# Storing GDN's Sm matrices as two transfers of 64 rows, with four Sm tiles

## The chip, the cores and the metric

The kernel runs on one core of one Trainium2 chip. The metric is device time in microseconds (us) for one execution. The kernel before has a median of 1775.48 us over three runs (1773.43 to 1786.22).

## The reference, cut to what matters

The reference is a two-layer trunk for a flow-matching generator: 256 latent tokens and 256 context tokens, model width 1024. Each layer runs four token mixers side by side (RWKV-7, gated DeltaNet or GDN, GLA and windowed attention), merges them by sigmoid gates, and ends with a SwiGLU. All of it is float32. The change touches GDN alone. For every chunk of 64 tokens, every head (four) and both directions GDN builds a strictly triangular matrix and solves with it:

```python
decay = jnp.exp(jnp.where(causal, gc[..., :, None] - gc[..., None, :], -jnp.inf))
lmat = jnp.where(strict, beta[..., :, None] * jnp.einsum('bnhid,bnhjd->bnhij', k, k) * decay, 0.0)
m = lmat + jnp.eye(c, dtype=F32)
u = lax.linalg.triangular_solve(m, v * beta[..., None], left_side=True, lower=True, unit_diagonal=True)
```

There are 512 tokens, so 8 chunks, 4 heads and 2 directions: 64 matrices of 64 x 64 in each layer. RWKV-7 is computed in the same chunked way and has matrices of the same size to invert.

## The kernel before, in words

Everything is issued by hand-written Python in program order, and a planner (the Tile layer) decides at build time in which order each engine runs its instructions. It goes by priorities: parts inside `high_priority(offset=20000)` come first, the gate projections (`w_gate`) are put late, to fill TensorE where other work waits. It also places tiles in memory pools. A tile with a tag has `bufs` slots; a new tile of that tag can only be written once the users of the slot's earlier tile are done, a DMA that reads it among them. At run time each engine works through its own list strictly in order, and so does SP, whose queue issues every DMA of this kernel. A wait at the head of a list holds all that stands behind it.

A layer runs RWKV (lines 372 to 600), then GDN (from line 625), with attention and GLA in the gaps. Beside them the dense projections run: each loads a 512 KB weight block `raw` (line 1111), ACT makes its rounded high part `whi`, DVE the rest `wlo`, and TensorE does 24 or so matmuls `pd` from both.

GDN's preparation makes the matrices in lines 740 to 764. Its outer loop runs over b, the pairs of heads. TensorE makes the Gram matrices of all eight chunks in one PSUM tile `pr` (traced as `m`), head p = 0 of the pair on partitions 0 to 63 and head p = 1 on 64 to 127. The inner loop runs over the direction d: DVE multiplies `pr` with minus beta into the tile `Sm` [128, 8, 64], then with the decays `At`. `Sm` has the tag "Sm" in the pool `gdt`, which has two slots for each tag. Four `Sm` tiles are made in each layer, in the order (b, d) = (0,0), (0,1), (1,0), (1,1). Line 764 then stores one tile to the DRAM scratch `dl`, whose dimensions are [j 64, d 2, p 2, b 2, n 8, i 64]. The stored access is `j p n i -> p j (n i)`: its first dimension is p with 2 steps, then j with 64, then 2 KB in a row. It is one transfer of 256 KB.

`tri_inverse` (lines 295 to 365) reads `dl` back in another order: two loads into `lx` (d = 0), two into `lt` (d = 1, line 314) and four into `bt` (line 318), in 32 x 32 blocks, one matrix to a lane. DVE then copies and runs 30 elimination steps on `lt` and `lx`, the result goes to DRAM and back as `TT`, and GDN's chain over the chunks (`gchain`, matmuls `psc`) uses it.

RWKV stores its matrices with the helper `tri_put` (line 291): `self.nc.sync.dma_start(out=st[0][:, d, p, b], in_=s)`. There s has the 64 partitions of one head, so the first dimension on both sides is j with 64 steps, again with 2 KB in a row: 128 KB for one transfer, 16 of them in the two layers.

Of the kernel before, what the change touches and what calls it, by code (L numbers as in the profile page):

```python
# [7 lines left out]
F32 = mybir.dt.float32  # L8
# [110 lines left out]
def bc(ap, shape, axis):  # L119
    return ap.unsqueeze(axis).to_broadcast(shape)  # L120


class Kern:
# [508 lines left out]
    def gdn(self, l, getp, misc, sg, y, full, other=lambda: None, fill=lambda: None, pre=None):  # L632
        nc, P, Q = self.nc, self.P, self.Q
        q0 = 0 if full else 256
        qs = 0 if full else 4
        with ExitStack() as es:
# [4 lines left out]
            tmp = self.pool("gdt", 2, es=e1, side="right")  # L641
# [15 lines left out]
            st = self.tri_begin()  # L657
# [41 lines left out]
            for p in range(2):  # L699
                for d in range(2):  # L700
                    nc.sync.dma_start(out=qi[64 * p:64 * p + 64, d].rearrange("p b t -> p (b t)"),
                                      in_=grd[p, d, 2 * d:2 * d + 2].rearrange("b n i -> (b n i)").partition_broadcast(64))
# [3 lines left out]
            for m in range(4):  # L706
                d = m % 2
# [37 lines left out]
            for b in range(2):  # L745
                for d in range(2):
                    EG = c3(qi[:, d, b])
                    Dd = At[:, d, b]
                    self.tt(Dd, EG, bc(GC[:, d, :, b], [128, 8, 64], 2), ALU.subtract)
                    self.act(EG, EG, ACTF.Exp)  # L750
                    nc.gpsimd.tensor_copy(el[:, d, b], EG[:, :, 63 if d == 0 else 0])
                    self.tt(c3(ke[:, d, b]), c3(QK[:, b, 0]), EG)
                    self.tt(Dd, Dd, bc(gmask[:, d], [128, 8, 64], 1), ALU.min)
                    self.act(Dd, Dd, ACTF.Exp)
                pr = self.ps().rearrange("p (n i) -> p n i", i=64)
                for n in range(8):
                    tk = slice(64 * n, 64 * n + 64)
                    for rw in rws:
                        self.mm(pr[rw, n], QK[rw, b, 0, tk], QK[rw, b, 0, tk])
                for d in range(2):  # L760
                    Sm = tmp.tile([128, 8, 64], F32, tag="Sm", name=self.nm("Sm"))
                    self.tt(Sm, pr, bc(nB[:, :, 2 * d + b], [128, 8, 64], 2))
                    self.tt(Sm, Sm, At[:, d, b])
                    nc.sync.dma_start(out=st[0][:, d, :, b].rearrange("j p n i -> p j (n i)"), in_=Sm.rearrange("p n i -> p (n i)"))
            next(inv)
            for b in range(2):
                conv(f"gq{b}", b, QK[:, b, 1, q0:T], q0)
# [78 lines left out]
            for s in range(8):  # L846
                with HP():
                    got = lockstep([link(s, d) for d in range(2)])
                for d in range(2):
                    n, U, So = got[d]  # L850
# [964 lines left out]
```

## Time and profile before

| | |
|---|---|
| median of three runs | 1775.48 us |
| the profiled execution | 1780.3 us, span 1778.5 us |
| TensorE (PE) busy | 1653.0 us, 93% of the span |
| VectorE (DVE) busy | 1097.3 us, 62% |
| ScalarE (ACT) busy | 831.2 us, 47% |
| mean granted TensorE clock | 0.961 of full speed |
| DMA queue 1 | 261.69 MB, 46.8% of 16 engines' span |

The span is cut into instructions per engine; PEld is the weight load of TensorE, which overlaps its matmuls. An idle stretch of an engine is put down to what ended it (the releaser). The chain of waits follows the end of the program back from each instruction to what released it. A DMA share is the mean busy share of the 16 DMA engines, so 0.06 is one engine and 1.00 all of them.

### The profile page before, as it was taken

To read this page: it belongs to the slowest core of one execution; us is meant where nothing else is said; L and a number is where in the kernel's file an instruction comes from. 1 tells how busy PE (TensorE), PEld (TensorE's weight loads), DVE (VectorE), ACT (ScalarE), POOL (GpSimd) and SP (SyncE) were. 2 spreads that over 40 slices of the span, in tenths; PEclk is the share of its full clock that TensorE was granted. 3 is DMA by queue.
4 is the path that set the end of the run, shared out by engine and by line. 5 is a ranking of instruction groups with operands and counts; after the bars stand their busy time and mean duration, and the time that the engine had idled before them with its cause. 6 is when DMAs were issued, how large, how long until landed. Compare 5 with 4: busy or idle time off the path is not lost. (4 is left out here: it accounts for less than half of the span.)

```text
span 1778.5 us, 31562 instructions
## 1 busy us (share of the span) xinstructions
PE 1653.0 (93%) x12480; PEld 1321.6 (74%) x12480; DVE 1097.3 (62%) x2243; ACT 831.2 (47%) x1440; POOL 144.1 (8%) x255
## 2 busy tenths in 40 slices
PE   6999999998998989999999999898999868889998
PEld 3776775666786667888878888777777766779986
DVE  3466643447935775899774226666577666766654
ACT  3665442355534235544433217763556432366653
POOL 0000111001001350000000000001021002400000
PEclk8999999998999999999999999998889877989999
DMA  9322554442452372566774223344532463445553
GB/s 338 119 96 90 157 151 164 150 146 78 140 146 90 94 239 90 186 222 216 242 236 153 95 95 107 102 127 136 162 98 97 127 167 103 142 143 187 183 201 118
DMA packets 149684, 263.71 MB, mean 148 GB/s; under 512 B 62224, under 2 KB 77088, under 8 KB 149408
## 3 DMA queue, kind: packets, MB, share of 16 engines
q1 hardware_dynamic: 149536, 261.69, 46.8%
q8 instruction: 98, 1.61, 0.4%
q14 instruction: 50, 0.41, 0.1%
HBM read 236.12 MB, written 25.53 MB: 147 GB/s over the span
## 5 line engine op out<-in xcount | busy, mean ns | idle before, releaser
L193 PE MATMUL pd<-hh,whi 128*128 128x512 f32 (+1 forms) x1648 | 550.8, 353 | 17.3 <-ACT g L171 5.2
L193 PE MATMUL pd<-hl,whi 128*128 128x512 f32 (+1 forms) x1648 | 545.5, 349 | 0.5 <-DVE hl L183 0.5
L183 DVE TENSOR_TENSOR wlo<-raw,whi 128x1024 fp32r<-128x1024 f32 x280 | 342.6, 1225 | 260.7 <-ACT whi L180 105.3
L180 ACT ACTIVATE whi<-raw 128x1024 fp32r<-128x1024 f32 x280 | 296.1, 1058 | 434.1 <-PE pd L193 251.9
L193 PEld LDWEIGHTS pd<-hh,whi 128*128 128x128 f32 x1648 | 317.1, 193 | 72.8 <-issue 9.2
L193 PEld LDWEIGHTS pd<-hl,whi 128*128 128x128 f32 x1648 | 317.2, 193 | 43.6 <-issue 6.1
L193 PE MATMUL pd<-hh,wlo 128*128 128x512 f32 (+1 forms) x1648 | 339.2, 345 | 4.9 <-DVE wlo L183 4.9
L193 PEld LDWEIGHTS pd<-hh,wlo 128*128 128x128 f32 x1648 | 263.5, 190 | 47.2 <-DVE wlo L183 5.3
L193 PE MATMUL t<-whi,ul 128*128 128x512 f32 x264 | 104.6, 396 | 0.0
L193 PE MATMUL t<-whi,uh 128*128 128x512 f32 x264 | 104.2, 395 | 0.0
L1258 DVE SCALAR_TENSOR_TENSOR gr<-gr,crow 128x512 f32<-128x512 f32 x112 | 75.5, 688 | 27.1 <-DMA gr<-in_ada_t_dram 26.1
L193 PE MATMUL t<-wlo,uh 128*128 128x512 f32 x264 | 75.3, 395 | 0.0
L171 ACT ACTIVATE g<-g 128x512 f32<-128x512 f32 (+1 forms) x128 | 66.6, 522 | 2.9
L183 DVE TENSOR_TENSOR th<-th,pd 128x512 f32<-128x512 f32 (+1 forms) x88 | 48.6, 552 | 29.2 <-PE pd L193 27.3
L183 POOL TENSOR_TENSOR acc<-acc,g 128x512 f32<-128x512 f32 (+1 forms) x48 | 57.5, 1215 | 60.7 <-DVE g L183 60.6
L193 PE MATMUL pd<-yp,whi 128*128 128x512 f32 (+1 forms) x192 | 54.0, 388 | 7.1 <-DVE g L183 3.5
L193 PEld LDWEIGHTS t<-whi,ul 128*128 128x128 f32 x264 | 49.7, 188 | 11.7
L193 PEld LDWEIGHTS t<-wlo,uh 128*128 128x128 f32 x264 | 49.7, 188 | 11.7
L193 PEld LDWEIGHTS t<-whi,uh 128*128 128x128 f32 x264 | 49.7, 188 | 11.4 <-DVE yr L183 0.2
L171 ACT ACTIVATE g<-pd,P 128x512 f32<-128x512 f32 (+1 forms) x64 | 36.9, 576 | 44.0 <-PE pd L193 33.1
L180 ACT ACTIVATE uh<-th 128x512 fp32r<-128x512 f32 (+1 forms) x44 | 23.1, 526 | 72.8 <-DVE th L183 72.7
L190 DVE SCALAR_TENSOR_TENSOR ac<-pp,P,ac 128x512 f32<-128x512 f32 (+1 forms) x72 | 52.2, 726 | 1.4 <-POOL UV L505 0.3
(366 smaller groups left out, 2241.1 us busy)
## 6 DMA issues: line engine op xcount, KB each, us to landing
raw<-in_ffn_w_dram SPq DMA_DIRECT2D x132, 512.0 KB, 3.3
raw<-in_w_gate_dram SPq DMA_DIRECT2D x64, 512.0 KB, 3.5
gr<-in_ada_t_dram SPq DMA_DIRECT2D x112, 256.0 KB, 3.4
raw<-in_w_in_dram SPq DMA_DIRECT2D x52, 512.0 KB, 3.3
raw<-in_ada_w_dram SPq DMA_DIRECT2D x40, 512.0 KB, 4.7
gd<-g SPq DMA_DIRECT2D x32, 256.0 KB, 3.2
raw<-in_w_branch_dram SPq DMA_DIRECT2D x16, 512.0 KB, 4.6
g<-gd SPq DMA_DIRECT2D x32, 256.0 KB, 4.2
```

The source lines that it names most:

```text
L171: return self.nc.scalar.activation(out=out, in_=in_, func=func, bias=bias, scale=scale, **kw)
L180: return self.nc.scalar.activation(out=out, in_=in_, func=ACTF.Copy, scale=scale)
L183: return (eng or self.nc.vector).tensor_tensor(out=out, in0=a, in1=b, op=op)
L190: return self.nc.vector.scalar_tensor_tensor(out=out, in0=a, scalar=s, in1=b, op0=op0, op1=op1)
L193: self.last = self.nc.tensor.matmul(out, lhsT=lhsT, rhs=rhs, start=start, stop=stop, skip_group_check=skip)
L1258: nc.vector.scalar_tensor_tensor(out=raw if v == nv - 1 else junk, in0=raw, scalar=1.0, in1=self.cr[:, v, 512 * h:512 * h + 512], op0=ALU. ...
```

## The change

Line 764 is replaced by two calls of RWKV's helper `tri_put`, one for each half of the partitions, so that a tile is stored by two transfers of 128 KB whose first dimension is j with 64 steps. The tag "Sm" gets four slots in place of two, so that all four tiles of a layer have memory of their own; a slot is 2 KB of each partition, and the pool `gdt` grows by 4 KB of each partition. The bytes stored, their places in DRAM and all arithmetic stay as they were. In the two layers 8 transfers become 16.

```diff
-                    Sm = tmp.tile([128, 8, 64], F32, tag="Sm", name=self.nm("Sm"))
+                    Sm = tmp.tile([128, 8, 64], F32, tag="Sm", name=self.nm("Sm"), bufs=4)
                     self.tt(Sm, pr, bc(nB[:, :, 2 * d + b], [128, 8, 64], 2))
                     self.tt(Sm, Sm, At[:, d, b])
-                    nc.sync.dma_start(out=st[0][:, d, :, b].rearrange("j p n i -> p j (n i)"), in_=Sm.rearrange("p n i -> p (n i)"))
+                    for p in range(2):
+                        self.tri_put(st, d, b, p, Sm[64 * p:64 * p + 64])
```

## Rows read from the trace of the kernel before

**Rows 1.** The page: busy time of the engines, and the whole chain by line.
```profile
PE 1653.0 (93%) x12480; PEld 1321.6 (74%) x12480; DVE 1097.3 (62%) x2243; ACT 831.2 (47%) x1440; POOL 144.1 (8%) x255
PE pd L193 12%; PE t L193 5%; PE m L193 2%; PE psc L193 2%; DMA dl<-Sm 1%; DVE wlo L183 1%; DVE lx L183 1%; DMA TT<-dx 1%; DVE lt L183 1%; PE S L193 1%; PE Y L193 0%; DMA dx<-lt 0%; PE O L193 0%; ACT whi L180 0%; SPq L336 0%
```

**Rows 2.** Chain of waits in layer 1: start us, length us, what held the end.
```profile
1391.72 10.57 DMA dl<-Sm
1402.32 0.69 DVE Sm L183
1403.97 9.29 DMA dl<-Sm
1413.68 2.74 DMA lt<-dl
```

**Rows 3.** By stretch: engines' busy us (x), granted PE clock, DMA share, GB/s.
```profile
428.00:430.00 2.00, 2.00 (x9) 1.56 (x10) 0.00 (x0) 0.15 (x1) 0.00 (x0) 1.00 0.13 51
438.00:440.00 2.00, 0.42 (x1) 0.43 (x2) 2.00 (x4) 0.63 (x1) 0.00 (x0) 0.50 0.13 51
1405.00:1407.00 2.00, 2.00 (x31) 1.78 (x32) 1.43 (x6) 0.00 (x0) 0.00 (x0) 0.50 0.13 51
1203.00:1205.00 2.00, 1.94 (x45) 1.63 (x40) 0.88 (x3) 1.76 (x4) 0.62 (x3) 1.00 0.92 304
```

**Rows 4.** The page's DMA issues: count, KB of one, us from issue to landing.
```profile
dl<-XL SPq DMA_DIRECT2D x16, 128.0 KB, 4.5
lx<-dl SPq DMA_DIRECT2D x8, 128.0 KB, 5.9
```

**Rows 5.** VectorE and SP in layer 0: start, us, operation [idle before <-releaser].
```profile
431.25 0.69 DVE L183 TENSOR_TENSOR Sm<-m,nB 128x512 f32<-128x512 f32 x1 [5.01 <-DMA dl<-Sm]
436.31 0.69 DVE L183 TENSOR_TENSOR Sm<-m,nB 128x512 f32<-128x512 f32 x1 [3.11 <-DMA dl<-Sm]
438.17 0.68 DVE L183 TENSOR_TENSOR QK<-tc,ac 128x512 f32<-128x512 f32 x1
423.20 15.57 SPq L764 DMA_DIRECT2D dl<-Sm  x4
446.54 0.91 SPq L314 DMA_DIRECT2D lt<-dl  x2
...
457.05 0.19 DVE L183 TENSOR_TENSOR lx<-lt 128x30 f32<-128x30 f32 x1
```

**Rows 6.** TensorE in layer 0, at full and at half clock.
```profile
419.13 1.02 PE L193 MATMUL m<-sq,c_ones 128*128 128x512 f32 x2
424.99 1.89 PE L193 MATMUL pd<-hh,wlo 128*128 128x512 f32 x7
439.57 2.08 PE L193 MATMUL m<-sq,c_ones 128*128 128x512 f32 x2 [7.38 <-ACT sq L171]
440.66 5.26 PE L193 MATMUL pd<-hh,wlo 128*128 128x512 f32 x12
```

**Rows 7.** VectorE and TensorE in layer 1.
```profile
1397.30 0.69 DVE L183 TENSOR_TENSOR Sm<-m,nB 128x512 f32<-128x512 f32 x1 [4.40 <-DMA dl<-Sm]
1402.32 0.69 DVE L183 TENSOR_TENSOR Sm<-m,nB 128x512 f32<-128x512 f32 x1 [2.53 <-DMA dl<-Sm]
1416.55 0.21 DVE L183 TENSOR_TENSOR lx<-lt 128x30 f32<-128x30 f32 x1 [0.92 <-DMA lt<-dl]
1399.66 0.58 PE L193 MATMUL pd<-hh,whi 128*128 128x256 f32 x1 [4.65 <-ACT g L171]
1401.75 0.41 PE L193 MATMUL pd<-hl,whi 128*128 128x256 f32 x1
1403.49 1.12 PE L193 MATMUL m<-QK 64*64 64x64 f32 x16 [1.32 <-DVE QK L190]
1406.38 2.47 PE L193 MATMUL m<-c_idn,v 64*64 64x64 f32 x64
1411.11 1.35 PE L193 MATMUL pd<-hh,wlo 128*128 128x256 f32 x10
...
1382.25 2.03 PE L193 MATMUL m<-c_idn,QK 64*64 64x64 f32 x64
1380.33 2.08 PE L193 MATMUL m<-QK 64*64 64x64 f32 x64
```

**Rows 8.** SP's queue in layer 1.
```profile
1389.21 3.03 SPq L764 DMA_DIRECT2D dl<-Sm  x2
...
1399.21 0.49 SPq L764 DMA_DIRECT2D dl<-Sm  x1
1407.81 2.29 SPq L314 DMA_DIRECT2D lx<-dl  x2
1433.28 15.08 SPq L1111 DMA_DIRECT2D raw<-in_w_branch_dram  x5
```

## The prediction

> **What bounds the kernel now.** I read the page first. TensorE is busy for 93% of the span and leads the chain of waits, and the store `dl<-Sm` has 1% of that chain, far more than eight transfers of 256 KB should need [rows 1]. So for most of the run the sum of the matmuls decides, and the change can only pay where TensorE stands still, or runs at a lower clock, because of this store. Second, the chain in order of time: in layer 1 it lies on the store for 10.57 us, then 9.29 us [rows 2]. Third, the table by stretches, to see why. In layer 0 and in layer 1 alike the DMA share stands at 0.13 while the four stores run, and 51 GB/s move [rows 3]. 0.13 of 16 engines is two engines. A tile of 262 KB at 51 GB/s takes 5.1 us, four of them 20.6 us, which fits the 20 us from the first issue at 423.2 us to the time at which layer 0's reads of `dl` can go on [rows 5]. The store's first dimension has two steps. RWKV's stores of the same kind of data, with 64 steps first, are landed 4.5 us after issue [rows 4], and the stretch with the last two of them moves 304 GB/s at a share of 0.92 (a weight block is among that traffic) [rows 3]. I conclude that the order of dimensions puts the store on two engines. Fourth, the instructions beside it: VectorE waits for a free Sm tile 5.01 and 3.11 us in layer 0 [rows 5], 4.40 and 2.53 us in layer 1 [rows 7]. What follows it on its list waits too, and so TensorE stands for 7.38 us in layer 0 [rows 6], 4.65 and 1.32 us in layer 1 [rows 7], and restarts at half clock (granted 0.50, the 1.2 GHz level, after it stood) [rows 3].
>
> **The change part by part.**
>
> *Four Sm tiles.* The third and fourth tile no longer wait for the stores of the first and second. VectorE's list moves up by 5.01 + 3.11 = 8.1 us in layer 0, and by 4.40 + 2.53 = 6.9 us in layer 1.
>
> Layer 0, TensorE: the matmul that ends the idle time waits for ScalarE's square of QK, and that for VectorE's QK at 438.17 us, which stands right behind the fourth Sm [rows 5]. 8.1 us earlier, its input is there before TensorE has finished what precedes it, so all 7.38 us go. Without the idle time there is no restart at half clock: the pair at 439.57 us took 2.08 us where the same pair took 1.02 at full clock, and twelve `pd` took 5.26 us where seven took 1.89, so 12 x 0.27 = 3.24 [rows 6]. That is 1.06 + 2.02 = 3.1 us more. 7.4 + 3.1 = 10.5 us for TensorE, 8.1 us for VectorE alone. TensorE is the engine that the following 50 us wait for, so I take 10 (the half microsecond is the extra issue below); bounds 6 (VectorE, and a quarter lost in a new order) and 12.
>
> Layer 1, TensorE: 4.65 + 1.32 = 6.0 us of idle time. At half clock, ten `pd`, the first at 1399.66 and the last at 1401.75 us, took 2.5 us against 1.35 for ten at 1411 us; 16 small matmuls took 1.12 us, twice, against 2.08 / 4 = 0.52; 64 took 2.47 against 2.03 [rows 7]. 1.15 + 1.2 + 0.44, and about 0.5 for five more `pd`, make 3.3 us; in all 9.3.
>
> *Two stores of 64 rows.* The inverse in layer 1 needs its two reads of `dl`. The third Sm would be done at 1394.8 us instead of 1399.2, when its store is issued now [rows 8]; two issues of 0.5 us and 4.5 us to landing [rows 4] give 1400.3 us for the reads of `lx`, which are issued at 1407.81 us now [rows 8]: 7.5 us earlier. The fourth Sm would be done 6.9 us earlier than its store starts now [rows 2], at 1397.0 us, its halves landed at 1402.5, and `lt`, issued at about 1413.3 us now (its landing is the next piece of the chain [rows 2]), goes 10.8 us earlier. The latest of three sets the start of the inverse, at 1416.55 us now [rows 7]: `lx` at 7.5 us, `lt` at 10.8, VectorE at 6.9 to 9.3 (its weight splits before the inverse follow TensorE). I take 8, with bounds 5 and 11. After it the inverse, the way back to `TT` and the chunk chain are one dependent line to the merge, with nothing tied to a clock time, so what is gained at its start arrives at the end; late next is `lx`, with 5.9 us from issue to landing [rows 4].
>
> In layer 0 the faster stores themselves are hidden: VectorE takes other work for several microseconds between the landing of `lt`, issued at 446.54 us, and the first elimination step at 457.05 us [rows 5]. They matter there by not taking the gain back: SP stands before the reads of `dl` and all weight loads queue behind it.
>
> *Four more issues in each layer.* Each is about 0.5 us of SP [rows 8]. SP waits for Sm at that point anyhow, which hides three; the last half lies on the path, 0.5 us in each layer, counted above. If SP were short of time there, it would be 2 us in each.
>
> *The pool grows by 4 KB of each partition.* No row shows its price; it moves the tiles behind it to other addresses and so to other earlier users. A tile already free costs nothing; the nearest row of a load held back by its tile is 15.08 us for five loads of `w_branch` [rows 8]. I take 0, since such waits in GDN's preparation are not seen before the first store, and keep +-4 us for this and for the planner's new order.
>
> **The sum**: 10 + 8 = 18 us. The profiled execution took 1780.3 us, 4.8 above the median, so it would take 1762.3, and the median 1775.5 - 18 = 1757.5. Bounds: 6 + 5 = 11 and 12 + 11 = 23 us, that is 1752.5 to 1764.5, with the new order's 4 us 1748.5 to 1768.5.
>
> **A rule against it.** The rows say that a store with 64 steps first runs wider than one with two [rows 3, 4]. The Trainium skill, page "DMA: Bandwidth & Descriptors", section "Rules for kernel authors", says of two transfers to disjoint partition halves "Don't bother", since they serialize on the same 16 engines, and wants one transfer of 128 partitions. By that rule the split alone would bring nothing and the time would come out as in the second rival, about 1774. The share of 0.13 speaks against applying it here: the one transfer that it prefers is on two engines, not on 16.
>
> **Rivals.**
> 1. *One layer pays.* The gain of one stage is taken back by its next wait, for instance in layer 1, where the loads of `w_branch` stand 15.08 us on SP for their tiles and the inverse's way back stands behind them in the same queue [rows 8]. For it: a fixed queue can be held by any of its members. Against it: those tiles are freed by VectorE's splits, which move up as well. Then 8 to 10 us remain: 1775.5 - 9 = 1766.5.
> 2. *The halves are no faster than the whole*, because the store is slow for another reason, such as two halves that run one after the other at the same 51 GB/s. Then the reads of `dl` stay where they are, SP holds the weight loads until then, and VectorE's earlier Sm only moves its wait to the reads: 1 or 2 us at most, 1774. For it: the tiles were stored in a row with no pause. Against it: RWKV's stores.
> 3. *Slower: a larger pool makes a tile wait.* Place: a load into GDN's or GLA's tiles on SP, ahead of the Sm stores or the weight loads. Price: 15 us in each layer by the row of 15.08 us [rows 8], 30 in all against 18 gained: 1787.5. It decides from 9 us a layer on; below that the kernel is still no slower than before. Against it: what lay at those addresses, RWKV's and attention's tiles, is mostly done by then.
>
> **How the numbers follow.** About 1%, 17.8 us, is what a measurement of this kernel can tell from no change. The forecast has 0.63, rival 1 0.19, rival 2 0.08, rival 3 0.05; 0.05 is left for a planner's order that gains more than 25 us. The forecast's own 18 us lies on the bound of 1%, so I give it two thirds above: 0.42 of 0.63, since the clock and the freed two engines add to it more easily than they take away. Faster 0.42 + 0.05 = 0.47; slower by over 1% is the worse half of rival 3 and a little for orders that I don't see, 0.04; the same 0.49. The range holds forecast and rival 1 and cuts off the outer ends: 1748 to 1772.
>
> **What would show it.** The stores of 128 KB land in 3 to 5 us and the share of 0.13 is gone. No wait of VectorE for `dl<-Sm` is left. TensorE has no idle stretch of 4 us or more between the Gram matmuls and the reads of `dl` in either layer, and its granted clock stays at 1.00. In layer 1 the first elimination step is 7 to 11 us nearer to the first Sm, now 27 us, from its store at 1389.21 us [rows 8] to 1416.55 [rows 7]. It is wrong if the halves take 5 us each at 51 GB/s, if VectorE waits at `lx` for as long as it waited at Sm, or if a load ahead of the stores now waits for its tile.

## The result and the profile after

The changed kernel takes 1756.26 us (median of four runs, 1748.81 to 1762.08), the kernel before, timed again with one more run, 1777.26 us. The ratio is 0.9869, 95% interval [0.9836, 0.9902]: 1.3% faster, 21 us by the medians. The forecast was 1757.5 us and 18 us. The profiled execution has a span of 1760.3 us, 18.2 less than the one of before.

The page of the changed kernel: busy time of the engines, then the whole chain by line.

```profile
PE 1653.4 (94%) x12480; PEld 1323.6 (75%) x12480; DVE 1094.8 (62%) x2243; ACT 832.0 (47%) x1440; POOL 143.3 (8%) x255
...
PE pd L193 43%; PE t L193 15%; PE m L193 8%; DMA gr<-in_ada_t_dram 3%; PE psc L193 3%; DVE wlo L183 2%; PE Y L193 2%; PE S L193 1%; PE O L193 1%; ACT whi L180 1%; DVE gr L1259 1%; DMA raw<-in_w_gate_dram 1%; PE h L196 1%; DMA g<-gd 1%; ACT D L171 1%
```

Against [rows 1] the engines do the same work in nearly the same busy time; only the span is shorter. `dl<-Sm` is gone from the lines of the chain. (The chain of before could be followed over a shorter part of the span, so the shares of the other lines are not to be compared.)

The changed kernel's instructions on Sm: count, duration in ns as least/median/greatest, first and last start; then who waited and the time to landing.

```profile
L293 SPq DMA_DIRECT2D dl<-Sm x16: 445/570/596, 426.7 to 1386.1; - x16
...
who waited for it (us, times):
busy tenths in 40 slices 0000000001000000000000000000000100000000
DMA to landing us min/median/max: 2.2/2.4/3.5
```

There are sixteen stores of 128 KB. Those whose landing the trace tells landed 2.2 to 3.5 us after their issue, and nobody waits for one.

By stretch in the changed kernel (columns as in rows 3): layer 0's stores and what follows them, then all of layer 1's stretch from the first Sm to the first elimination step.

```profile
430.00:440.00 10.00, 10.00 (x42) 7.50 (x41) 9.90 (x15) 6.98 (x12) 0.16 (x3) 1.00 0.91 158
440.00:450.00 10.00, 10.00 (x96) 7.61 (x95) 9.90 (x16) 6.84 (x11) 0.26 (x3) 1.00 0.26 99
...
1371.00:1395.00 24.00, 23.98 (x327) 22.80 (x324) 21.12 (x35) 15.22 (x28) 4.87 (x5) 1.00 0.57 122
```

The even share of 0.13 [rows 3] is gone. In layer 0 TensorE is busy for all 20 us from 430 to 450 us at a granted clock of 1.00, where it stood for 7.38 us and restarted at half clock [rows 6]. In layer 1 TensorE is busy for 23.98 of 24 us at a granted clock of 1.00, where it stood for 4.65 and 1.32 us and restarted at half clock [rows 7, 3].

SP and VectorE in layer 1 of the changed kernel: start, us, operation [idle before <-releaser].

```profile
1378.70 3.60 SPq L293 DMA_DIRECT2D dl<-Sm  x4
...
1384.29 2.36 SPq L293 DMA_DIRECT2D dl<-Sm  x4
...
1388.26 1.04 SPq L314 DMA_DIRECT2D lx<-dl  x2
1389.40 1.44 SPq L314 DMA_DIRECT2D lt<-dl  x2
```
```profile
1371.02 2.48 DVE L183 TENSOR_TENSOR Sm<-m,nB 128x512 f32<-128x512 f32 x4 [2.40 <-PE m L193]
...
1394.15 1.09 DVE L320 COPY lt<-lx 64x1024 f32<-64x1024 f32 x1
1395.28 0.21 DVE L183 TENSOR_TENSOR lx<-lt 128x30 f32<-128x30 f32 x1
```

From the first store to the first elimination step it is 16.6 us now (1378.70 to 1395.28), 27.3 before (1389.21 to 1416.55, [rows 8, 7]). The step carries no wait for a transfer any more: what stands before it on VectorE's list is its own weight splits.

The span, cut at instructions that both traces have (starts in us; XL is RWKV's tile of such matrices):

| from the start of | before | after | stretch before | stretch after | difference |
|---|---|---|---|---|---|
| the span to the first Sm | 0 | 0 | 421.3 | 424.8 | +3.5 |
| first Sm, layer 0, to the first product of its SwiGLU | 421.3 | 424.8 | 303.1 | 290.0 | -13.1 |
| that, to RWKV's last XL, layer 1 | 724.4 | 714.8 | 478.4 | 481.2 | +2.8 |
| that, to the first Sm, layer 1 | 1202.8 | 1196.0 | 178.7 | 175.0 | -3.7 |
| that, to the first elimination step | 1381.5 | 1371.0 | 35.0 | 24.3 | -10.7 |
| that, to the chunk chain (first `psc`) | 1416.5 | 1395.3 | 59.8 | 58.0 | -1.8 |
| that, to the end | 1476.3 | 1453.3 | 302.2 | 307.0 | +4.8 |

The gain lies in the two stretches around the stores. The other rows sum to +5.6 us, and the changed kernel profiled a second time (e8 below) differs from its first profile by as much in them: 477.9 us in place of 481.2 up to RWKV's last XL, 301.1 in place of 307.0 at the end. In the two stretches of the gain it has 292.9 and 24.3 us. In the last stretch of the first profile 96 matmuls of the output projection take 24.2 us instead of 22.4, at a granted clock of 0.83 from 1528 to 1540 us.

### The profile page after: what moved, and what is told of

Same layout as the page of the kernel before. It is cut to its first block, busy times and chain, and to the rows that moved or that the text cites. A ratio compares the mean times of both kernels' runs of the same rounds, so it can differ in the third digit from the quotient of the medians.

```text
span 1760.3 us, 31581 instructions
## 1 busy us (share of the span) xinstructions
PE 1653.4 (94%) x12480; PEld 1323.6 (75%) x12480; DVE 1094.8 (62%) x2243; ACT 832.0 (47%) x1440; POOL 143.3 (8%) x255
## 4 chain that ended last, share of the span: by engine, by line
PE 75%; DVE 10%; DMA 6%; ACT 5%; issue 3%; POOL 1%; SPq 1%; DVEq 0%; ACTq 0%; POOLq 0%
PE pd L193 43%; PE t L193 15%; PE m L193 8%; DMA gr<-in_ada_t_dram 3%; PE psc L193 3%; DVE wlo L183 2%; PE Y L193 2%; PE S L193 1%; PE O L193 1%; ACT whi L180 1%; DVE gr L1259 1%; DMA raw<-in_w_gate_dram 1%; PE h L196 1%; DMA g<-gd 1%; ACT D L171 1%
## 5 line engine op out<-in xcount | busy, mean ns | idle before, releaser
L193 PEld LDWEIGHTS pd<-hh,whi 128*128 128x128 f32 x1648 | 316.9, 193 | 68.4 <-issue 10.5
L193 PEld LDWEIGHTS t<-whi,ul 128*128 128x128 f32 x264 | 49.6, 188 | 12.1
```

Source lines behind the costliest of these rows:

```text
L193: self.last = self.nc.tensor.matmul(out, lhsT=lhsT, rhs=rhs, start=start, stop=stop, skip_group_check=skip)
```

## The experiments

All ratios are against the kernel before, timed on the same chip in five rounds.

**e1: four tiles, one store each.**
```diff
-Sm = tmp.tile([128, 8, 64], F32, tag="Sm", name=self.nm("Sm"))
+Sm = tmp.tile([128, 8, 64], F32, tag="Sm", name=self.nm("Sm"), bufs=4)
```


> Four Sm tiles, each still stored by one transfer whose first dimension has two steps. Theory (the store is slow because it runs on two engines): the share stays at 0.13 and 51 GB/s, four stores still need about 20 us in each layer, VectorE's waits for a free Sm go, but the reads of dl are issued no earlier than before (about 18 us after the first store) and VectorE or SP waits there instead; 0 to 6 us faster than before. Rival (the two tile slots were the cost, the rate of the store does not matter): all of the change's gain, about 20 us faster, ratio 0.987.

Ratio 1.0011 [0.9986, 1.0037]: nothing. By stretch in layer 0 of this kernel, then VectorE's and TensorE's waits (layer 0 at 451.85 and 454.19 us, layer 1 from 1384.46):

```profile
436.00:440.00 4.00, 4.00 (x16) 2.62 (x15) 3.90 (x6) 3.34 (x6) 0.00 (x0) 1.00 0.13 51
448.00:452.00 4.00, 0.00 (x0) 0.00 (x0) 0.15 (x1) 0.00 (x0) 0.00 (x0) 0.76 0.40 80
```
```profile
451.85 1.02 DVE L320 COPY lt<-lx 64x1024 f32<-64x1024 f32 x1 [8.98 <-DMA lx<-dl]
...
1384.46 2.49 DVE L183 TENSOR_TENSOR Sm<-m,nB 128x512 f32<-128x512 f32 x4 [0.94 <-PE m L193]
...
1417.75 1.02 DVE L320 COPY lt<-lx 64x1024 f32<-64x1024 f32 x1 [11.14 <-DMA lx<-dl]
1419.59 0.20 DVE L183 TENSOR_TENSOR lx<-lt 128x30 f32<-128x30 f32 x1 [0.82 <-DMA lt<-dl]
```
```profile
454.19 2.07 PE L193 MATMUL m<-sq,c_ones 128*128 128x512 f32 x2 [8.64 <-ACT sq L171]
```

The waits for Sm are gone, the 51 GB/s are not, and the wait reappears at the next user of the data: 8.98 us in layer 0 and 11.14 in layer 1, before the copy of `lx`, where Sm had cost 8.1 and 6.9 [rows 5, 7]. TensorE stands for 8.64 us in place of 7.38, before the same pair of matmuls [rows 6].

In layer 1 this kernel's VectorE has the same operations in the same order as the changed kernel's, from the four products of Sm in a row to the first elimination step. It takes 35.1 us here (1384.46 to 1419.59) and 24.3 there (1371.02 to 1395.28); only the stores differ.

**e2: two stores of 64 rows, two tiles.**
```diff
-nc.sync.dma_start(out=st[0][:, d, :, b].rearrange("j p n i -> p j (n i)"), in_=Sm.rearrange("p n i -> p (n i)"))
+for p in range(2):
+    self.tri_put(st, d, b, p, Sm[64 * p:64 * p + 64])
```


> Two stores of 64 rows, but two Sm tiles as before. Theory: a store lands 2.4 to 3.5 us after its issue, so the third and fourth Sm wait 0 to 2 us each in place of 2.5 to 5.0, and the reads of dl go early; 15 to 20 us faster than before. Rival (the slots were the cost): VectorE still waits for each store and most of the gain is missing, 0 to 6 us faster.

Ratio 0.9869 [0.9829, 0.9909], the same as the whole change. The Sm instructions of this kernel:

```profile
L293 SPq DMA_DIRECT2D dl<-Sm x16: 445/587/1552, 429.6 to 1388.3; - x16
...
who waited for it (us, times):
busy tenths in 40 slices 0000000001000000000000000000000100000000
DMA to landing us min/median/max: 2.2/2.4/3.3
```

With two slots there is no wait either: the planner put other work of VectorE between the second and the third tile, and the stores have landed by then. The faster stores bring all of the gain; the four tiles add nothing that can be measured.

**e3: two stores of a tile, cut along the chunks** (with four tiles; a row is 1 KB here and 2 KB in the change).
```diff
+for h in range(2):
+    hn = slice(4 * h, 4 * h + 4)
+    nc.sync.dma_start(out=st[0][:, d, :, b, hn].rearrange("j p n i -> p j (n i)"), in_=Sm[:, hn].rearrange("p n i -> p (n i)"))
```


> Four Sm tiles and two stores of 128 KB for each tile as in the change, but cut along the chunks (n), so that the first dimension of each store still has two steps and a row is 1 KB. Theory (the first dimension decides): 0.13 and 51 GB/s as before, four tiles in 20 us, total within 3 us of four tiles with one store each. Rival (two smaller transfers run side by side, their number decides): the stores of a tile land in 3 us and the time is that of the change, about 20 us faster than before.

Ratio 1.0005 [0.9979, 1.0032]. By stretch while the stores run in this kernel, and its issues on SP:

```profile
428.00:430.00 2.00, 2.00 (x11) 1.61 (x10) 2.00 (x3) 1.49 (x3) 0.14 (x2) 1.00 0.14 48
430.00:432.00 2.00, 2.00 (x10) 1.65 (x9) 2.00 (x4) 1.85 (x3) 0.00 (x0) 1.00 0.14 48
```
```profile
422.97 15.91 SPq L766 DMA_DIRECT2D dl<-Sm  x8
441.75 2.87 SPq L314 DMA_DIRECT2D lx<-dl  x2
```

The same number and size of transfers as in the change, and still two engines at 48 GB/s, with the reads of `lx` 18.8 us after the first store. So it is not the number or the size of the transfers that confines them; their first dimension still has two steps. (The profiled execution took 1769.40 us, the median of the twelve is 1776.12: a single execution does not rank kernels that are 10 us apart.)

**e4: four stores of 32 rows** (the edit is against the change).
```diff
 for p in range(2):
-    self.tri_put(st, d, b, p, Sm[64 * p:64 * p + 64])
+    for r in range(2):
+        o = 64 * p + 32 * r
+        nc.sync.dma_start(out=st[0][32 * r:32 * r + 32, d, p, b], in_=Sm[o:o + 32])
```


> The change with each half cut once more: four stores of 32 rows (64 KB) for a tile, 16 in a layer. Theory (the first dimension, 32, is still wide, and SP has time while VectorE makes the tiles): stores land in 2 to 3 us, eight more issues of 0.55 us cost at most 2 us in each layer, 16 to 20 us faster than before. Rival (SP's issues lie on the path): 4.4 us more in each layer, 11 us faster than before.

Ratio 0.9885 [0.9845, 0.9925]. The issues on SP in layer 0, and the time to landing:

```profile
429.48 8.71 SPq L767 DMA_DIRECT2D dl<-Sm  x16
438.29 1.01 SPq L314 DMA_DIRECT2D lx<-dl  x2
```
```profile
DMA to landing us min/median/max: 1.6/1.7/3.3
```

Twice the issues cost nothing that can be measured: SP has time while VectorE makes the tiles.

**e5 and e6: one layer alone** (the condition is `full`, true in layer 0, and its opposite).
```diff
+Sm = tmp.tile([128, 8, 64], F32, tag="Sm", name=self.nm("Sm"), bufs=4 if full else 2)
+if full:
+    for p in range(2):
+        self.tri_put(st, d, b, p, Sm[64 * p:64 * p + 64])
+else:
+    ...
```


> The change in the first layer alone; the second keeps one store for a tile and two tiles. Theory (each layer's store holds its own layer): 8 to 13 us faster than before, ratio 0.993 to 0.995, the first projection of the first layer's SwiGLU about 10 us earlier, and in the second layer VectorE still waits 4.4 and 2.5 us for Sm and the inverse starts 27 us after the first store. Rival (one layer pays): the whole 20 us or nothing.

> The change in the second layer alone. Theory: 8 to 12 us faster than before, ratio 0.993 to 0.995; together with the first layer alone about 20 us. In the first layer TensorE still stands 7 us while VectorE waits for Sm. Rival (one layer pays): the complement of the first layer alone, nothing or 20 us.

Layer 0 alone: 0.9941 [0.9920, 0.9962], 10.5 us of 1775.16. Layer 1 alone: 0.9932 [0.9914, 0.9949], 12.1 us. The product is 0.9873; the whole change beside them (e8) gave 0.9880. VectorE where the change was left out, first layer 1 of e5, then layer 0 of e6:

```profile
1376.49 0.69 DVE L183 TENSOR_TENSOR Sm<-m,nB 128x512 f32<-128x512 f32 x1 [4.45 <-DMA dl<-Sm]
1381.51 0.69 DVE L183 TENSOR_TENSOR Sm<-m,nB 128x512 f32<-128x512 f32 x1 [2.53 <-DMA dl<-Sm]
1395.91 0.21 DVE L183 TENSOR_TENSOR lx<-lt 128x30 f32<-128x30 f32 x1 [1.11 <-DMA lt<-dl]
```
```profile
431.47 0.69 DVE L183 TENSOR_TENSOR Sm<-m,nB 128x512 f32<-128x512 f32 x1 [5.02 <-DMA dl<-Sm]
436.52 0.69 DVE L183 TENSOR_TENSOR Sm<-m,nB 128x512 f32<-128x512 f32 x1 [3.10 <-DMA dl<-Sm]
```

Each layer's waits stand as they were [rows 5, 7], and each layer pays for itself.

**e7: Sm planned early, and e8: the change again.**
```diff
+with self.tc.high_priority(offset=20000):
     for b in range(2):
         ...
         Sm = tmp.tile([128, 8, 64], F32, tag="Sm", name=self.nm("Sm"), bufs=4)
```


> The change, and the loop that makes and stores Sm planned at high priority, ahead of the gate projections beside it. Theory (after the change the inverse's start is set by VectorE's weight splits and the order around Sm, no longer by the store): the inverse can start 2 to 6 us earlier in the second layer, up to 4 us faster than the change, ratio to before 0.984 to 0.989. Rival (TensorE's matmuls bound the stage now): no faster than the change or some us slower, 0.987 to 0.992.

> The changed kernel as it is, timed beside the three others on this chip: ratio to before 0.984 to 0.991. It is the sum against which the two single layers are held, and the base for the early Sm.

e8: 0.9880 [0.9859, 0.9901]. e7: 0.9875 [0.9853, 0.9897]. In the profiles the end of the inverse (the copy into `lx` after the last step), counted from RWKV's last XL in layer 1, comes after 235.6 us (1188.0 to 1423.6); in the two profiles of the changed kernel it is 238.8 (e8, 1193.9 to 1432.7) and 237.0 us (1196.0 to 1433.0). That is hardly more than those two differ by, and the time does not show it. No version that I tried beats the change.

**e9: one wide store of 128 rows.** With the head p outermost in the scratch, p and j are one dimension of 128 steps. A lane's 32 matrices are then no longer in one even row, so each read into `lx` and `lt` is cut in two, RWKV's too.
```diff
-self.dram.tile([64, 2, 2, 2, 8, 64], F32, name=self.nm("dl"))
+self.dram.tile([2, 64, 2, 2, 8, 64], F32, name=self.nm("dl"))
...
-nc.sync.dma_start(out=t[lane(d, q)], in_=blk(dl, d, q, q))
+for p in range(2):
+    r = (2 * d + q) * L + 16 * p
+    nc.sync.dma_start(out=t[r:r + 16], in_=dl[p, q_of(q), d, :, :, q_of(q)].rearrange("j b n i -> (b n) j i"))
...
+nc.sync.dma_start(out=st[0][:, :, d, b].rearrange("p j n i -> (p j) (n i)"), in_=Sm.rearrange("p n i -> p (n i)"))
```


> Four Sm tiles and one store of 128 rows for each tile again, but into a scratch laid out with the head p outermost, so that p and j are one dimension of 128 steps; the reads into lx and lt are cut in two for that, 8 in place of 4 in each of the four inversions. Theory (the first dimension decides, not the number of transfers): the share of 0.13 is gone, one store lands in 3 to 4 us, and the time is that of the change, ratio to before 0.985 to 0.990, less up to 2 us for each inversion by the added reads (0.5 us each on SP). Rival (the halves themselves are the gain): 51 GB/s and the time of before.

Ratio 1.0025 [1.0006, 1.0044]: as slow as before, against my theory's time, and yet the store did what the theory said:

```profile
L766 SPq DMA_DIRECT2D dl<-Sm x8: 319/326/395, 441.7 to 1404.3; - x8
...
DMA to landing us min/median/max: 2.1/2.4/3.9
```

The first Sm comes late already: 338.7 us after RWKV's first XL (101.0 to 439.7), in the changed kernel 320.9 (103.9 to 424.8). From RWKV's last XL in layer 1 to the last Sm it is 188.2 us against 188.8. So about 18 us are lost before GDN in layer 0, where only the scratch's layout, the cut reads and the order planned around them differ. VectorE at the start of RWKV's inverse there, first in this kernel, then in the changed one:

```profile
195.71 1.10 DVE L322 COPY lt<-lx 64x1024 f32<-64x1024 f32 x1
203.19 1.22 DVE L183 TENSOR_TENSOR wlo<-raw,whi 128x1024 fp32r<-128x1024 f32 x1 [6.38 <-PE pd L193]
208.76 1.22 DVE L183 TENSOR_TENSOR wlo<-raw,whi 128x1024 fp32r<-128x1024 f32 x1 [4.34 <-PE pd L193]
209.91 0.20 DVE L183 TENSOR_TENSOR lx<-lt 128x30 f32<-128x30 f32 x1
```
```profile
192.13 1.10 DVE L320 COPY lt<-lx 64x1024 f32<-64x1024 f32 x1
197.54 1.23 DVE L183 TENSOR_TENSOR wlo<-raw,whi 128x1024 fp32r<-128x1024 f32 x1 [4.32 <-ACT whi L180]
198.68 0.20 DVE L183 TENSOR_TENSOR lx<-lt 128x30 f32<-128x30 f32 x1
```

The first elimination step comes 108.9 us after the first XL in e9 and 94.8 us after it in the changed kernel (94.7 or 94.8 in every other profile of this case), and no transfer holds it: SP issues the reads from 181.90 to 188.42 us, in 6.5 us (6.2 in the changed kernel). Ahead of the step VectorE's list has one weight split more, and each split waits for TensorE's products. From 200 to 240 us TensorE is then busy for 29.6 us, in the changed kernel for 38.9. So 14 of the 18 us lie in the planned order, not in the added reads. The profile also lacks the gain of GDN in layer 0: from the first Sm to the SwiGLU it takes 299.5 us (290.0 in the changed kernel). Together that is some 27 us, and the timed ratios are 26 us apart (1.0025 against 0.9880).

**e10: the same in GDN alone**, RWKV with its own scratch and reads as in the change.
```diff
+wide = dl.shape[0] == 2
...
-st = self.tri_begin()
+st = (self.dram.tile([2, 64, 2, 2, 8, 64], F32, name=self.nm("dl")), self.tri_begin()[1])
```


> As the one wide store of 128 rows, but the scratch with the head outermost and the cut reads in GDN alone; RWKV keeps its stores, reads and so its planned order. Theory (what the one wide store lost lay in RWKV's inversions, where first Sm came 18 us later than in the changed kernel, and one wide store is as good as two halves): VectorE reaches the first Sm at 420 to 426 us as before, a store lands in 2.4 us, and the time is that of the change, ratio 0.985 to 0.991. Rival (one store or the cut reads cost the time in GDN itself): 1.000 or more.

Ratio 0.9891 [0.9866, 0.9915], the change's within the intervals. The Sm instructions of this kernel:

```profile
L770 SPq DMA_DIRECT2D dl<-Sm x8: 319/323/333, 423.1 to 1387.3; - x8
...
DMA to landing us min/median/max: 2.1/2.5/4.2
```

The first Sm is back at 421.2 us. One store of 256 KB lands in the time of one of 128 KB, and in layer 1 the first elimination step comes 23.2 us after the first Sm (1372.8 to 1396.0), 24.3 in the changed kernel. In e9, then, RWKV's part lost the time.

In layer 0, however, the profiled stretch from the first Sm to the SwiGLU is 300.0 us (421.2 to 721.2), near the kernel before. Two of SP's waits in it and TensorE's:

```profile
SPq L232 <- DVE ac L190: 17.1, 1, 17.1
SPq L1117 <- DVE lx L183: 12.3, 1, 12.3
```
```profile
477.16 0.79 PE L193 MATMUL pd<-hh,whi 128*128 128x512 f32 x1 [5.96 <-ACT lqk L180]
```

The stores and reads are issued by 436 us. Later SP stands 17.1 us with the load of a mask and 12.3 us with a weight block, both until an operation of VectorE is done, and TensorE stands for 5.96 us. So the planned order gives much of the gain back there. The time of e10 lies at the change's all the same; the intervals of e10 and e8 leave room for a loss of some 10 us (0.9859 to 0.9915), and I did not settle it further.

## Why the prediction was right

*The bound.* Right: the store ran on two engines because its first dimension had two steps. e3 keeps number and size of the transfers and stays at 48 to 51 GB/s; e10 keeps one transfer with rows of 2 KB, makes the first dimension wide, and its stores land as fast as the halves. The Trainium skill, page "DMA: Bandwidth & Descriptors", section "Why a DMA increments its semaphore by 16 and not by 1", has the rule behind it: the engines that a transfer uses are the largest number up to 16 that divides the slowest dimension of both sides. The share of 0.13, two of 16, agrees with it.

*The rule against it* does not apply here, as forecast. The Trainium skill, page "DMA: Bandwidth & Descriptors", section "Rules for kernel authors", says "Don't bother" because both halves spread over all 16 engines anyway, and the one store here used two: the halves gained 1.2 to 1.3%. As far as the rule says that halves are no better than one transfer, e10 bears it out (0.9891 against 0.9880), but only once the one transfer is wide. Rival 2 falls with e2 and e3.

*Four tiles and two stores.* The terms were split wrongly, though their sum held. I gave VectorE's 8.1 and 6.9 us, and what TensorE gains by them, to the four tiles. e1 shows that they bring nothing alone, and e2 that they bring nothing beside the halves. The two waits are one delay, the 20 us of the store, seen at two places: at the next Sm, or at the reads. That the faster stores "matter there by not taking the gain back", as the step on layer 0 says, is what e1 shows, with 8.98 us taken back; that they are hidden there was wrong. So layer 0's 10 us came out in part by luck: TensorE's idle time and its restart at half clock, which it counts, did go, but by the stores and not by the tiles.

*A reading.* The prediction lets layer 0's reads go on 20 us after the first store. The trace has the first read of `lx` on SP at 441.47 us and that of `lt` at 446.54, 18.3 and 23.3 us after it; the argument stands on either.

*The sizes.* Layer 0: forecast 10 with bounds 6 and 12, by e5 10.5. Layer 1: forecast 8 with bounds 5 and 11, by e6 12.1 (9.1 to 15.3 by its interval), of which 10.7 stand in the profile up to the first elimination step. The undersized term was layer 1's start of the inverse. I took 8 as the latest of three: 7.5 for `lx`, with 4.5 us for a store to land, 10.8 for `lt`, and 6.9 to 9.3 for VectorE. The stores land in 2.4 us, and `lx` holds nothing up: before VectorE's copy of `lx` at 1394.15 us stand its own splits. The two prices rested on little. In the trace of before, least, median and greatest landing are all 4.5 us for RWKV's stores and all 5.9 us for the reads of `lx`, a single landing each; in the changed kernel the same stores take 2.3 to 5.1 us, the same reads 3.9 by their median.

*The extra issues* are hidden (e4). *The larger pool* costs nothing that can be measured: with it alone the ratio is 1.0011 (e1), and without it the halves are as fast (e2), so rival 3 falls. *Rival 1* falls with e5 and e6: both layers pay, and the sum comes through to the end.

*The chances.* The gain of 21 us lies above the bound of 1%. The prediction had put 0.47 on that and 0.49 on less than 1% either way, so it did not favour what came.

## What to carry to other kernels

Look for stretches in which the DMA share stands still at a low value while a transfer runs; here it was 0.13, two engines of 16. Read the transfer's first dimension on both sides. Here a leading dimension of two was worth a second transfer or another layout, and the number of transfers cost little because the issuing queue had time. When a wait for a slow transfer is removed by more buffers, ask who reads the data next: the wait goes there.

A few more transfers can also change the planned order. In e9 that cost RWKV 14 us at a place where no transfer was waited for, so look at what stands ahead of a late instruction on its engine's list before the transfer is blamed.

## What the runs showed of the hardware

Two DMA engines moved 48 to 51 GB/s (the kernel before, e1, e3). A store of 128 rows with one merged first dimension is issued in 0.32 us on SP (e10), one of 64 rows in 0.57 us (the changed kernel), and the narrow one took 0.5 us as well [rows 8]. Landing took 2.1 to 4.2 us for 256 KB (e10), 2.2 to 3.5 us for 128 KB (the changed kernel) and 1.6 to 3.3 us for 64 KB (e4).
